# A two-layer hybrid decoder trunk in float32: split weight pairs kept in HBM, token shift on ScalarE, a quarter rope table, and a planner with other durations

## The chip, the cores and the metric

One core of a Trainium2 chip runs the whole program in one launch. The metric is the device time of one execution in microseconds (us). TensorE is called PE here, VectorE DVE, ScalarE ACT, GpSimd POOL; SP is the sync engine, which issues every DMA of this kernel, in one queue and in order.

## The reference

The input is x of 1024 tokens by 1024 features. Each of two layers does this:

```
h = rms_norm(x, g1)
pa, pb, pc = split(h @ w_in)          # 1024 -> 1056 + 768 + 448 columns
ya = rwkv7_mixer(pa)     # pa + (shift(pa) - pa) * mu, then a delta-rule recurrence over the tokens
yb = dilated_mixer(pb)   # rope on 16 of 64 features of q and k, three dilations, softmax
yc = mla_mixer(pc)       # low-rank q and kv, rope on 64 features, causal softmax
x = x + concat(ya, yb, yc) @ w_out
h = rms_norm(x, g2)
x = x + (silu(h @ w_gate) * (h @ w_up)) @ w_down
```

`shift` moves every feature one token later, with zero ahead of the first token. The rope tables are the cosine and the sine of position times a frequency: 8 frequencies for mixer B, 32 for mixer C, and the 8 of B are every fourth one of the 32 of C. A last norm follows the second layer.

## The kernel before, in words

Activations lie with features on the 128 partitions and half of the tokens (`HALF` = 512) along a row, so that a tile ("page", from a pool of 79) is 128 x 512 float32. A float32 product is made of three passes in the PE's faster float32r form (`mm3`): each operand is split into a high part (`wh`, by an ACT copy that rounds) and a low part (`wl` = value minus high part, by POOL or DVE), and high x high, high x low and low x high are summed in PSUM.

**Weights.** A weight matrix is read in units of 128 x 512 (256 KB), each worth 4 x 3 matmuls of 512 columns. `loader` has two strands: `fetch` reads raw units ahead (at most 3, `NRAW`), and the main loop splits them by `split(wr, wh, wl, "pool")` into a ring of 6 pairs (`NW`); `drop` gives a pair back when its last matmul has been emitted. The input projection (18 column blocks of two units, `in_items`) and the output projection (8 blocks of two units, `out_items`) are run for each half of the tokens, `hf` 0 and 1, and for each half every unit is read and split anew: 36 and 16 units per half and layer.

**The mixers.** `in_proj` runs the blocks of hf 0, then those of hf 1, and hands each block's PSUM bank on: `shifted` (blocks 0 to 8) does the token shift, `evac_to` the rest. In `shifted` ACT copies the bank to `raw` (in layer 0, hf 0 DVE does it with the norm's factor), then DVE makes `last - raw` for one column, `raw` shifted minus `raw` for 511 columns, and a scalar_tensor_tensor with `mu`. `recurrence(hf)` is a long serial chain over 8 chunks of 64 tokens that goes back and forth between PE, DVE and ACT: first an elimination of 31 steps (`Wp`, `tmp`, two small DVE operations each) between 32 x 1024 transposes on DVE (`vtrans`), which PE's `mg` matmuls wait for; then, chunk by chunk, `X` (PE), `Xs` (DVE), `U` (PE), `UV` (ACT), `Hp` (PE). The attention of B and C runs beside it and after it. Then come the output projection (`wo`) and the feed-forward part (`gu`, `dn`), which are long runs of 512-column matmuls.

**Rope.** `rope_tables(kind, hf)` makes cosine and sine on 128 x 512 for one kind of rope and one half; `all_rope` runs it four times, in layer 0, from the end of hf 0 on, and stores the four pairs in `rope_dram`. `load_rope` reads a pair back by two DMAs.

**Order.** All of this is written as Python generators ("strands"). A planner (`Flow`) picks the next instruction to emit by simulated clocks: `F.op(engine, cost)` advances an engine's clock by the planner's price of an operation, and `LATENCY` (150 ns after DVE, ACT or POOL, 230 ns after PE, 130 ns more where PE is the one that waits) is added from an operation to the next of its strand. Engines run their instructions in the order of emission, so a price that is off puts an instruction too early or too late in its engine's queue; SP's DMAs come in that order too. Prices before: a DVE operation of n columns costs 1.04 n + 65 ns, a DVE transpose 1.1 n + 65, an ACT copy 0.833 n + 80, POOL 2.2 n + 65, a float32r matmul max(n, 2m) x 0.4167 + 3, a float32 one 4 max(n, m) x 0.4167 + 6.

Of the kernel before, what the change touches and what calls it, by code (L numbers as in the profile page):

```python
# [18 lines left out]
L = 2  # L19
T = 1024  # L20
# [61 lines left out]
class Strand:  # L82
# [148 lines left out]
def trunk(ctx: ExitStack, tc: tile.TileContext, xT, pos, vec, con, first, w_in, small, uq, uqr, ukv,  # L231
# [45 lines left out]
    def activation(out, in_, func, bias=None, scale=None, accum_out=None):  # L277
        cost = cols(in_) * 0.833 + 80
        kw = {}
        for k, v in (("bias", bias), ("scale", scale), ("accum_out", accum_out)):  # L280
            if v is not None:
                kw[k] = v
                if not isinstance(v, float):
                    cost += 93
# [7 lines left out]
    def acopy(out, in_):  # L292
        F.op("act", cols(in_) * 0.833 + 80)
# [4 lines left out]
    def tt(eng, out, a, b, op):  # L298
        F.op(eng, cols(out) * (1.04 if eng == "dve" else 2.2) + 65)
        ENG[eng].tensor_tensor(out=out, in0=a, in1=b, op=op)  # L300

    def ts(out, in_, s1, s2, op0, op1=None, rate=0.55):
        F.op("dve", cols(out) * rate + 65)
# [3 lines left out]
    def stt(out, a, s, b, op0, op1):  # L307
        F.op("dve", cols(out) * 1.04 + 65)
        nc.vector.scalar_tensor_tensor(out=out, in0=a, scalar=s, in1=b, op0=op0, op1=op1)  # L309

    def vcopy(out, in_, rate=1.04):
        F.op("dve", cols(out) * rate + 65)
        nc.vector.tensor_copy(out=out, in_=in_)

    def recip(out, in_):
        F.op("dve", cols(out) * 8.33 + 65)
# [129 lines left out]
    afix = {"last": fix.tile([128, 9], F32, name="last")}  # L446
# [5 lines left out]
    rope_dram = drp.tile([2, 2, 2, 128, HALF], F32, name="rope_dram")  # L452
# [3 lines left out]
    rope_done = [[Event(), Event()] for _ in range(2)]  # L456
# [15 lines left out]
    raws, ring = Slots(NRAW), Slots(NW)  # L472
    at_layer = [0]

    def loader(items):

# [18 lines left out]
        queue = [(k, parts(k, srcs), own(k)) for k, srcs in items]  # L495
# [19 lines left out]
        for k, todo, keep in queue:  # L515
            if k[0] == "S":
# [13 lines left out]
            F.set(W[k], (wh, wl))  # L530
# [190 lines left out]
    def rope_tables(kind, hf):  # L721

        col = CON["rope"] + 3 * kind
        s = P["gp"]
# [4 lines left out]
        F.cur.last, F.cur.t = None, dma(q, pos[0:1, hf * HALF:(hf + 1) * HALF].partition_broadcast(128), 262144)  # L729
        yield "dve"  # L730
        vcopy(ang, q)
        free(q)
        yield "dve"
        ts(ang, ang, cons[:, col:col + 1], None, ALU.mult)
        yield "dve"
        ts(k, ang, 0.15915494309189535, 12582912.0, ALU.mult, ALU.add)
        yield "dve"
        ts(k, k, -12582912.0, None, ALU.add)
        for c in (-6.28125, -1.93500518798828125e-3, -3.0199157663e-7):
            yield "dve"  # L740
            stt(ang, k, c, ang, ALU.mult, ALU.add)
        yield "dve"
        ts(ang, ang, 3.1415925, -3.1415925, ALU.min, ALU.max)
        yield "act"
        activation(k, ang, ACTF.Sin)
        yield "dve"
        ts(k, k, cons[:, col + 1:col + 2], None, ALU.mult)
        yield "dma"
        t = dma(rope_dram[kind, hf, 1], k, 262144)
        free(k)  # L750
        yield "dve"
        stt(ang, ang, -1.0, ang, ALU.mult, ALU.max)
        yield "dve"
        ts(ang, ang, -1.0, 1.5707963267948966, ALU.mult, ALU.add)
        yield "act"
        activation(ang, ang, ACTF.Sin)
        yield "dma"
        t = dma(rope_dram[kind, hf, 0], ang, 262144)
        free(ang)
        F.set(rope_done[kind][hf], None, t)  # L760

    def all_rope():
        for kind in range(2):
            for hf in range(2):
                yield from rope_tables(kind, hf)

    def load_rope(kind, hf, where, ev, keep=0):
        yield rope_done[kind][hf]
        C, S = yield from pages(where, ["ropeC", "ropeS"], keep=keep)
        yield "dma"  # L770
        dma(C, rope_dram[kind, hf, 0], 262144)
        F.set(ev, (C, S), dma(S, rope_dram[kind, hf, 1], 262144))
# [25 lines left out]
    def group(g, where, scale, mask, score, vpass, emit_out, whole, later, end):  # L798
# [5 lines left out]
        def qtile(i4):  # L804
# [9 lines left out]
            for cc in range(nch):  # L814
                n = ns[cc]
                yield "dve"
                F.op("dve", n * 1.04 + 65)
# [149 lines left out]
    def layer(l):  # L967
# [67 lines left out]
        def shifted(hf, idx, p, r0=0, r1=128):  # L1035
            yield Need([rawa])
            raw = yield from page(["gp"], "raw", keep=room(1) if hf else 0)
            yield from evac(raw[r0:r1], p[r0:r1], hf, slice(r0, r1))
            if idx != 8:
                free(p)  # L1040
            if hf == 1:
                yield A[0][idx]
            last = afix["last"][r0:r1, idx:idx + 1]
            m = yield from page(["gp"], "pa", keep=room(1) if hf else 0)
# [5 lines left out]
            yield "dve"  # L1050
            stt(m[r0:r1], m[r0:r1], vcol(l, "mu", idx)[r0:r1], raw[r0:r1], ALU.mult, ALU.add)
            free(raw)
# [41 lines left out]
        def in_proj():  # L1094
            for hf in range(2):
                order = IN_ORDER[hf]
                for n_, idx in enumerate(order):
                    if hf == 0 and n_ == 4:
                        F.spawn(norm1(1), 4)
                    if l == 0 and (hf, n_) == ROPE_START:  # L1100
                        F.spawn(all_rope(), 7)
# [74 lines left out]

        def start_a():
            nc.vector.memset(afix["last"], 0.0)
# [32 lines left out]
        def recurrence(hf):  # L1211
# [88 lines left out]
            for j in range(2):  # L1300
# [13 lines left out]
                F.op("dve", 1130)  # L1314
# [1325 lines left out]
```

## Time and profile before

| | us |
|---|---|
| runs | 2668.68, 2671.2, 3381.49 |
| median | 2671.2 |
| the profiled execution's own time | 2675.43 |
| its span, first to last instruction | 2673.5 |
| PE busy in it | 2564.4 (96%) |
| DVE, POOL, ACT busy | 1822.3, 1269.6, 1154.0 |
| mean granted PE clock | 0.97 |
| moved by DMA | 365.09 MB, 137 GB/s |

The busy time of PE counts modelled ends of pipelined matmuls, so a stretch can be 100% busy without running at full pace; PEld is the time in which weights are loaded into PE's array, one load to a matmul. The granted clock has two levels here, 1.0 (2.4 GHz) and 0.5 (1.2 GHz); a row gives its mean over a stretch.

### The profile page before, as it was taken

The numbers are of one execution on the slowest core, as the hardware profiler recorded it, in microseconds if no ns is written. First come the engines' busy times: TensorE is split into PE (matmuls) and PEld (weight loads), VectorE is DVE, ScalarE is ACT, GpSimd is POOL, SyncE is SP. The second block draws the span as 40 slices with busy tenths as digits, with TensorE's granted clock in tenths as the row PEclk, the third lists the DMA queues.
The fourth block names the chain that finished last, engine by engine and source line by source line (L and its number), as shares of the span: only waits on it lengthen the run. The fifth ranks groups of instructions, "written<-read, shape, count | busy, mean of one in ns | idle before, by whom it ended". The sixth has DMA issues, their size and how long they took to land. (4 is left out here: it accounts for less than half of the span.)

```text
span 2673.5 us, 38613 instructions
## 1 busy us (share of the span) xinstructions
PE 2564.4 (96%) x13112; PEld 2053.2 (77%) x13112; DVE 1822.3 (68%) x3535; ACT 1154.0 (43%) x2319; POOL 1269.6 (47%) x978
## 2 busy tenths in 40 slices
PE   7999898999999999999999999999998999999998
PEld 5777765688777888888877778658887888888887
DVE  7978648674778666655578377677548876665556
ACT  5354346564433433332354434756634333333221
POOL 4635433146664444356564255213656444454660
PEclk9889888999999999999999998999999999999999
DMA  5231202015435443698342221111352554349851
GB/s 185 81 115 60 79 20 70 18 60 193 155 115 204 168 141 131 242 347 286 123 143 81 72 74 50 46 35 59 114 200 95 190 173 165 124 149 348 285 205 63
DMA packets 204773, 365.09 MB, mean 137 GB/s; under 512 B 23712, under 2 KB 38304, under 8 KB 204448
## 3 DMA queue, kind: packets, MB, share of 16 engines
q1 hardware_dynamic: 204576, 362.63, 39.8%
q8 instruction: 103, 1.69, 0.3%
q14 instruction: 94, 0.77, 0.1%
HBM read 253.22 MB, written 105.64 MB: 134 GB/s over the span
## 5 line engine op out<-in xcount | busy, mean ns | idle before, releaser
L300 POOL TENSOR_TENSOR wl<-wr,wh 128x512 fp32r<-128x512 f32 (+1 forms) x376 | 550.6, 1476 | 459.8 <-ACT wh L294 410.2
L265 PE MATMUL gu<-hhi,wh 128*128 128x512 f32 x1232 | 483.3, 393 | 18.6 <-ACT u L294 12.6
L265 PE MATMUL gu<-hhi,wl 128*128 128x512 f32 x1232 | 480.7, 391 | 1.2 <-POOL wl L300 1.0
L265 PE MATMUL gu<-hlo,wh 128*128 128x512 f32 x1232 | 481.2, 391 | 0.0
L294 ACT CAST wh<-wr 128x512 fp32r<-128x512 f32 (+1 forms) x496 | 287.2, 597 | 104.8 <-POOL wl L300 35.3
L265 PEld LDWEIGHTS gu<-hhi,wh 128*128 128x128 f32 x1232 | 232.3, 189 | 76.5 <-ACT u L294 15.1
L265 PEld LDWEIGHTS gu<-hhi,wl 128*128 128x128 f32 x1232 | 232.4, 189 | 51.1 <-POOL wl L300 2.5
L300 POOL TENSOR_TENSOR wl<-s,wh 128x512 fp32r<-128x512 f32 (+1 forms) x136 | 180.1, 1333 | 187.6 <-ACT wh L294 84.1
L265 PEld LDWEIGHTS gu<-hlo,wh 128*128 128x128 f32 x1232 | 232.4, 189 | 47.3
L265 PE MATMUL dn<-bhi,wh 128*128 128x512 f32 (+1 forms) x664 | 251.7, 380 | 0.7 <-issue 0.7
L265 PE MATMUL dn<-blo,wh 128*128 128x512 f32 (+1 forms) x664 | 251.5, 379 | 0.0
L265 PE MATMUL dn<-bhi,wl 128*128 128x512 f32 (+1 forms) x664 | 251.5, 379 | 0.0
L265 PE MATMUL inp<-hhi,wh 128*128 128x512 f32 x512 | 219.2, 428 | 9.3 <-ACT wh L294 9.3
L294 ACT CAST wh<-s 128x512 fp32r<-128x512 f32 (+1 forms) x204 | 116.7, 581 | 229.8 <-DVE s L300 199.7
L265 PE MATMUL inp<-hhi,wl 128*128 128x512 f32 x512 | 209.1, 408 | 0.3 <-POOL wl L300 0.3
L265 PE MATMUL inp<-hlo,wh 128*128 128x512 f32 x512 | 209.0, 408 | 0.0
L300 DVE TENSOR_TENSOR x<-x,dn 128x512 f32<-128x512 f32 (+1 forms) x160 | 104.4, 657 | 110.6 <-PE dn L265 82.1
L300 DVE TENSOR_TENSOR v<-u,gu 128x512 f32<-128x512 f32 x132 | 89.9, 682 | 127.8 <-PE gu L265 125.4
L300 POOL TENSOR_TENSOR v<-v 128x512 f32<-128x512 f32 x66 | 97.1, 1474 | 136.7 <-DVE v L300 126.4
L265 PEld LDWEIGHTS dn<-bhi,wh 128*128 128x128 f32 x664 | 124.9, 188 | 25.2 <-issue 1.5
L265 PEld LDWEIGHTS dn<-bhi,wl 128*128 128x128 f32 x664 | 124.9, 188 | 23.6
L265 PEld LDWEIGHTS dn<-blo,wh 128*128 128x128 f32 x664 | 124.9, 188 | 23.1
(316 smaller groups left out, 5500.8 us busy)
## 6 DMA issues: line engine op xcount, KB each, us to landing
wr<-in_w_in_dram SPq DMA_DIRECT2D x144, 256.0 KB
act_dram<-ahi SPq DMA_DIRECT2D x142, 256.0 KB
act_dram<-alo SPq DMA_DIRECT2D x142, 256.0 KB
bhi<-act_dram SPq DMA_DIRECT2D x142, 256.0 KB
blo<-act_dram SPq DMA_DIRECT2D x142, 256.0 KB
wr<-in_w_gate_dram SPq DMA_DIRECT2D x104, 256.0 KB
wr<-in_w_up_dram SPq DMA_DIRECT2D x104, 256.0 KB
wr<-in_w_down_dram SPq DMA_DIRECT2D x96, 192.0 KB
```

The source lines that it names most:

```text
L265: nc.tensor.matmul(out=out, lhsT=lhsT, rhs=rhs, start=start, stop=stop, **kw)
L294: nc.scalar.copy(out=out, in_=in_)
L300: ENG[eng].tensor_tensor(out=out, in0=a, in1=b, op=op)
```

## The change

Four things are done together.

1. **Weight pairs.** When a unit of `w_in` or `w_out` has been split for hf 0, both parts are also written to HBM (`pairs_dram`); for hf 1 they are read from there, straight into the ring, with no raw tile and no split.
2. **Token shift.** ACT reads the PSUM bank twice, times (1 - mu) and times mu (in hf 1 already moved by one column), and DVE adds the two. `last` holds mu times the last column. The vector `less` = 1 - mu is made once per layer in place of a memset.
3. **Rope table.** One table for 32 frequencies x 4 blocks of 256 tokens on 128 partitions: cosine, sine and minus sine. `load_rope` gathers both kinds from it, by 8 DMAs in place of 2; for B, POOL first fills the pages with 1 and 0.
4. **Planner prices.** New durations for every operation, and 35 ns in place of 150 from an operation to the next of its strand on the same engine.

```diff
         if self.last is None or (self.last == "pe" and self.want == "pe"):
             return self.t
+        if self.last == self.want:
+            return self.t + 35.0
         return self.t + LATENCY[self.last] + (EXTRA if self.want == "pe" else 0.0)
...
         if lhsT.dtype == F32R:
-            F.op("pe", max(n, 2 * m) * 0.4167 + 3)
+            F.op("pe", max(n + 32, 262) * 0.4167)
         else:
-            F.op("pe", 4 * max(n, m) * 0.4167 + 6)
+            F.op("pe", 2 * max(n + 20, m) * 0.4167 + 4)
...
     def acopy(out, in_):
-        F.op("act", cols(in_) * 0.833 + 80)
+        F.op("act", cols(in_) * 0.833 + 175)
...
     def tt(eng, out, a, b, op):
-        F.op(eng, cols(out) * (1.04 if eng == "dve" else 2.2) + 65)
+        F.op(eng, cols(out) * 1.2 + 150 if eng == "dve" else cols(out) * 2.5 + 120)
...
     def vtrans(out, in_):
-        F.op("dve", cols(in_) * 1.1 + 65)
+        F.op("dve", cols(in_) * 1.9 + 150)
...
+    def again(k):
+        return k[0] in ("in", "wo") and k[2] == 1
...
-        queue = [(k, parts(k, srcs), own(k)) for k, srcs in items]
+        queue = [(k, [] if again(k) else parts(k, srcs), own(k)) for k, srcs in items]
...
         for k, todo, keep in queue:
+            if again(k):
+                yield there[(*k[:2], 0, *k[3:])]
+                yield Need([ring])
+                w = yield from pages(["gp"], ["wh", "wl"], F32R, keep, 3.2)
+                at = pair(k)
+                yield "dma"
+                for i in range(2):
+                    t = dma(f32(w[i]), at[i], 262144)
+                F.set(W[k], w, t)
+                continue
...
             yield from split(wr, wh, wl, "pool")
             raw_free(wr)
-            F.set(W[k], (wh, wl))
+            now = F.cur.at()
+            if k[0] in pairs_dram:
+                yield "dma"
+                for i, w in enumerate((wh, wl)):
+                    t = dma(pair(k)[i], f32(w), 262144)
+                F.set(there[k], None, t)
+            F.set(W[k], (wh, wl), now)
...
-    def rope_tables(kind, hf):
+    def rope_tables():
...
+        col, n = CON["rope"] + 3, T // 4
...
+        C, S, N, q_ = ang[:, 0:n], k[:, 0:n], k[:, n:2 * n], q[:, 0:n]
         yield "dma"
+        for b in range(4):
+            t = dma(q_[32 * b:32 * b + 32], pos[0:1, b * n:(b + 1) * n].partition_broadcast(32), 32768)
...
+        for i, a in enumerate((C, S, N)):
+            t = dma(rope_dram[i], a, 131072)
...
+        if kind == 0:
+            for t, v in ((C, 1.0), (S, 0.0)):
+                yield "pool"
+                F.op("pool", 550)
+                nc.gpsimd.memset(t, v)
...
+        for i, a in enumerate(starts):
+            for t, v in ((C, src[0]), (S, src[1 if i % 2 else 2])):
+                done = dma(t[a:a + n].rearrange("p (q t) -> p q t", q=2), v, 2048 * n)
...
         def shifted(hf, idx, p, r0=0, r1=128):
...
+            d, m = yield from pages(["gp"], ["raw", "pa"], keep=room(1) if hf else 0)
+            src = p
+            if not (hf or l):
+                yield from evac(d[r], p[r], hf, r)
...
+            yield "act"
+            activation(m[r], src[r], ACTF.Copy, scale=rest)
...
+            yield "act"
+            if hf:
+                activation(d[r, 1:], src[r, 0:HALF - 1], ACTF.Copy, scale=mu)
+                acopy(d[r, 0:1], last)
+            else:
+                activation(d[r], src[r], ACTF.Copy, scale=mu)
+                acopy(last, d[r, HALF - 1:])
...
             yield "dve"
-            tt("dve", m[r0:r1, 0:1], last, raw[r0:r1, 0:1], ALU.subtract)
-            tt("dve", m[r0:r1, 1:], raw[r0:r1, 0:HALF - 1], raw[r0:r1, 1:], ALU.subtract)
-            if hf == 0:
-                vcopy(last, raw[r0:r1, HALF - 1:])
-            yield "dve"
-            stt(m[r0:r1], m[r0:r1], vcol(l, "mu", idx)[r0:r1], raw[r0:r1], ALU.mult, ALU.add)
-            free(raw)
+            if hf:
+                tt("dve", m[r], m[r], d[r], ALU.add)
+            else:
+                tt("dve", m[r, 1:], m[r, 1:], d[r, 0:HALF - 1], ALU.add)
+            free(d)
```

## Rows read from the trace of the kernel before

**Rows 1.** The page, engines' busy time (share of the span) and instructions:

```profile
PE 2564.4 (96%) x13112; PEld 2053.2 (77%) x13112; DVE 1822.3 (68%) x3535; ACT 1154.0 (43%) x2319; POOL 1269.6 (47%) x978
```

**Rows 2.** Busy time by stretch; last columns: granted clock, DMA share, GB/s:

```profile
core 0: us, PE busy (x) PEld busy (x) DVE busy (x) ACT busy (x) POOL busy (x), PEclk, DMA share, GB/s
14.00:160.00 146.00, 135.37 (x659) 110.32 (x658) 134.34 (x261) 64.45 (x107) 81.82 (x61) 0.95 0.36 123
160.00:400.00 240.00, 221.45 (x1608) 170.73 (x1607) 157.43 (x377) 108.44 (x211) 96.09 (x80) 0.88 0.18 59
400.00:620.00 220.00, 204.81 (x1046) 151.22 (x1045) 156.85 (x457) 139.06 (x344) 76.82 (x77) 0.95 0.17 54
620.00:700.00 80.00, 80.00 (x360) 66.37 (x359) 40.30 (x57) 34.55 (x61) 49.72 (x37) 1.00 0.63 211
1330.00:1900.00 570.00, 548.67 (x3312) 423.14 (x3311) 402.13 (x1018) 293.73 (x638) 242.59 (x210) 0.96 0.22 69
```

**Rows 3.** Waits of PE: who waited for whom, total us, times, longest:

```profile
PE mg L265 <- DVE T1Y L321: 9.3, 2, 8.2
...
PE hsum L275 <- DVE sq L313: 8.5, 7, 3.5
PE U L265 <- DVE Xs L313: 6.1, 5, 2.6
...
PE gu L265 <- POOL wl L300: 1.0, 1, 1.0
```

**Rows 4.** The same stretches view, 20 us around the longest of these waits:

```profile
290.00:300.00 10.00, 4.87 (x33) 4.33 (x31) 8.06 (x23) 2.12 (x4) 2.85 (x3) 0.85 0.79 265
300.00:310.00 10.00, 6.96 (x118) 6.56 (x119) 5.52 (x7) 2.11 (x4) 1.78 (x1) 0.50 0.08 16
```

**Rows 5.** DVE groups of the rope tables, costliest and cheapest of 8, 44 instructions:

```profile
L309 DVE SCALAR_TENSOR_TENSOR ang<-kr,ang 128x512 f32<-128x512 f32 x12 | 9.1, 762 | 0.0
...
L313 DVE CAST ang<-posi 128x512 f32<-128x512 int32 x4 | 1.7, 415 | 0.0
```

**Rows 6.** Groups of the token shift (busy us, mean ns | idle before):

```profile
L309 DVE SCALAR_TENSOR_TENSOR pa<-pa,vecs,raw 128x512 f32<-128x512 f32 (+1 forms) x36 | 35.4, 986 | 0.3
L300 DVE TENSOR_TENSOR pa<-raw 128x511 f32<-128x511 f32 (+1 forms) x36 | 25.6, 710 | 0.0
L300 DVE TENSOR_TENSOR pa<-last,raw 128x1 f32<-128x1 f32 (+1 forms) x36 | 15.1, 419 | 13.3 <-ACT raw L294 13.1
L294 ACT COPY raw<-inp 128x512 f32<-128x512 f32 (+1 forms) x27 | 15.8, 584 | 31.6 <-PE inp L265 31.5
```

**Rows 7.** Groups of the weight split on POOL and ACT, and a DVE transpose:

```profile
L300 POOL TENSOR_TENSOR wl<-wr,wh 128x512 fp32r<-128x512 f32 (+1 forms) x376 | 550.6, 1476 | 459.8 <-ACT wh L294 410.2 <-DVE x L300 17.4 <-issue 10.8
L294 ACT CAST wh<-wr 128x512 fp32r<-128x512 f32 (+1 forms) x496 | 287.2, 597 | 104.8 <-POOL wl L300 35.3 <-PE dn L265 18.5 <-POOL x L300 18.1
L321 DVE STREAM_TRANSPOSE TT<-W 32x1024 f32<-32x1024 f32 x8 | 18.3, 2287 | 2.5 <-ACT W L294 2.5
```

**Rows 8.** Timeline of SP, one DMA issue: start us, us:

```profile
24.09 0.40 SPq L328 DMA_DIRECT2D swt<-in_small_dram  x1
```

**Rows 9.** DMA issues of the input projection's weights, count and size:

```profile
wr<-in_w_in_dram SPq DMA_DIRECT2D x144, 256.0 KB
```

**Rows 10.** The stretches view again, where DMA is busiest in the projections:

```profile
20.00:30.00 10.00, 7.17 (x37) 5.84 (x38) 7.14 (x19) 3.75 (x9) 3.66 (x3) 1.00 0.76 269
30.00:40.00 10.00, 9.91 (x48) 8.00 (x46) 9.89 (x15) 6.68 (x12) 7.78 (x6) 1.00 1.05 384
620.00:640.00 20.00, 20.00 (x90) 16.57 (x89) 10.27 (x11) 10.88 (x20) 14.08 (x10) 1.00 0.78 275
```

**Rows 11.** Waits of SP's queue, 160 to 300 us, then 1450 to 1700 us:

```profile
SPq L328 <- DVE kr L305: 59.6, 3, 22.6
SPq L328 <- DVE yA L300: 18.9, 1, 18.9
...
SPq L328 <- PE Yp L265: 25.9, 1, 25.9
SPq L328 <- DVE yA L300: 25.3, 2, 22.8
```

More of the change, by code (lines that the diff above doesn't have):

```diff
@@ L298, in tt @@
     def tt(eng, out, a, b, op):
-        F.op(eng, cols(out) * (1.04 if eng == "dve" else 2.2) + 65)
+        F.op(eng, cols(out) * 1.2 + 150 if eng == "dve" else cols(out) * 2.5 + 120)
         ENG[eng].tensor_tensor(out=out, in0=a, in1=b, op=op)
     def ts(out, in_, s1, s2, op0, op1=None, rate=0.55):
-        F.op("dve", cols(out) * rate + 65)
+        F.op("dve", cols(out) * rate + 180)
         kw = {} if op1 is None else {"op1": op1}
@@ L445, in trunk @@
     pj_dram = drp.tile([10, 128, HALF], F32, name="pj_dram")
-    afix = {"last": fix.tile([128, 9], F32, name="last")}
+    afix = {"last": fix.tile([128, 9], F32, name="last"), "less": fix.tile([128, 9], F32, name="less")}
     for i in range(2):
@@ L455, in trunk @@
     xs_done = [[Event(), Event()] for _ in range(KD)]
-    rope_done = [[Event(), Event()] for _ in range(2)]
+    rope_done = Event()
     flip = [0]
@@ L472, in trunk @@
     raws, ring = Slots(NRAW), Slots(NW)
+    pairs_dram = {"in": drp.tile([L, 18, 2, 2, 128, HALF], F32, name="pairs_in"),
+                  "wo": drp.tile([L, KD, 2, 2, 128, HALF], F32, name="pairs_wo")}
     at_layer = [0]
+    def again(k):
+        return k[0] in ("in", "wo") and k[2] == 1
+    there = {}
     def loader(items):
+        there.update({k: Event() for k, _ in items if k[0] in pairs_dram})
         def keep(k):
@@ L493, in parts, with pair @@
             return [(Event(), srcs[g][b], g, b) for g, b in at]
[L495 removed]
+        def pair(k):
+            return pairs_dram[k[0]][k[1], k[3], k[4]]
+        queue = [(k, [] if again(k) else parts(k, srcs), own(k)) for k, srcs in items]
         def fetch():
@@ L750, in rope_tables @@
-        free(k)
-        yield "dve"
[L752 to L756, printed above, removed]
-        yield "dma"
[L758 to L772, printed above, removed]
+        stt(C, C, -1.0, C, ALU.mult, ALU.max)
+        yield "dve"
+        ts(C, C, -1.0, 1.5707963267948966, ALU.mult, ALU.add)
+        yield "act"
+        activation(C, C, ACTF.Sin)
+        yield "dve"
@@ new lines, in rope_tables, with load_rope @@
+        ts(N, S, -1.0, None, ALU.mult)
+        yield "dma"
+        for i, a in enumerate((C, S, N)):
+            t = dma(rope_dram[i], a, 131072)
+        free(ang, k)
+        F.set(rope_done, None, t)
+    def load_rope(kind, hf, where, ev, keep=0):
+        yield rope_done
+        C, S = yield from pages(where, ["ropeC", "ropeS"], keep=keep)
+        rows = slice(64 * hf, 64 * hf + 64)
+        if kind == 0:
[3 more added lines that the diff above has]
+                nc.gpsimd.memset(t, v)
+            src = [rope_dram[i, rows].rearrange("(q g r) t -> r g q t", q=2, r=4)[0] for i in range(3)]
+            n, starts = 8, (0, 8, 64, 72)
+        else:
+            src = [rope_dram[i, rows].rearrange("(q f) t -> f q t", q=2) for i in range(3)]
+            n, starts = 32, (0, 32, 64, 96)
+        yield "dma"
+        for i, a in enumerate(starts):
+            for t, v in ((C, src[0]), (S, src[1 if i % 2 else 2])):
+                done = dma(t[a:a + n].rearrange("p (q t) -> p q t", q=2), v, 2048 * n)
+        F.set(ev, (C, S), done)
@@ L1175, in open_a @@
             F.set(a_open)
+        less = afix["less"]
         def start_a():
-            nc.vector.memset(afix["last"], 0.0)
+            o = l * NVEC + VEC["mu"]
+            ts(less, vecs[:, o:o + 9], -1.0, 1.0, ALU.mult, ALU.add)
         def load_swt():
```

57 lines of the change are left out of this document (28 added, 29 removed).

## The prediction

> **What bounds the kernel now.** I read the page's busy times first, then the stretches, then who makes PE wait, and last the groups that the change touches. The page shows PE busy in 2564.4 of 2673.5 us [rows 1]: at most 109.1 us are plain idle, and no other engine is near full. The stretches tell where. In 620 to 700 us (the output projection) PE has no idle time, runs at clock 1.00 and does 360 matmuls in 80 us, 222 ns each [rows 2]; that is its pace when it is fed. The two mixer stages are different. In layer 0 (14 to 620 us) PE idles 606 - 561.6 = 44.4 us, and the clock of 0.95, 0.88 and 0.95 takes another 146 x 0.05 + 240 x 0.12 + 220 x 0.05 = 47.1 us of full pace; in layer 1 (1330 to 1900 us) it is 21.3 us idle and 570 x 0.04 = 22.8 us by the clock [rows 2]. Together the mixers lose 65.7 + 69.9 = 135.6 us. The other 43.4 us of idle time lie at the start, at the two entries of the feed-forward part and in the last norm, which the change hardly touches. So what can be won is a part of 135.6 us, or 5%, and nothing that only lightens POOL or ACT wins by itself.
>
> The Trainium skill, "Perfetto Trace Analysis", section "Identifying the Most-Contended Engine", says that matmul busy time is a poor measure of the room left and that the share of weight loading is a better one. Here that share is 66.37 / 80 = 0.83 where PE is fed; at this share the loads of the two mixer stages would fill 521 of 606 and 510 of 570 us, a room of 145 us against 65.7 by the idle time [rows 2]. By it a third of the room is 48 us, by the idle time alone 22.
>
> The waits show what the loss is made of. PE's `mg` waits 9.3 us for the elimination's last DVE transpose, `hsum` 8.5 us for a DVE copy, `U` 6.1 us for `Xs` on DVE; a split `wl` on POOL makes `gu` wait 1.0 us [rows 3]. Around the longest wait PE is busy in only 4.87 of 10 us, and the next 10 us run at 0.50 [rows 4]: one wait of 8.2 us is paid again at half clock. PE's loss in the mixers is mostly lateness of DVE's links in the recurrence, met by matmuls that stand too early in PE's queue.
>
> **The change, part by part.** The sum is made against the profiled execution, 2675.4 us, which is 4.2 us above the median of the runs (2671.2).
>
> *Rope table.* Out go 44 DVE instructions in eight groups, of which the first and the last are shown; the eight sum to 30.1 us [rows 5]. In come 11 on 256 columns; each is priced at the cheapest row's 415 ns at most, so 4.6 us. DVE gains 25.5 us, nearly all in 160 to 400 us. PE loses (18.6 + 28.8) / 240 = 20% of that stretch [rows 2]; taking DVE's time to be on the path in that share gives 5 us. Ends: 0 (the strand has the lowest priority and fills gaps) and 25.5. DMAs: 4 position loads, 8 stores and 16 loads become 4, 3 and 64, 43 more issues of 0.40 us [rows 8], 17 us of SP's time spread over two layers; SP is not on the path and the weights' lead hides them, so I take 0, with 17 as the end if the lead is gone. Eight fills on POOL, even at the 1476 ns of a split, make 12 us [rows 7] on an engine that is busy 40% of that stretch: 0.
>
> *Token shift.* A shift takes 0.986 + 0.710 + 0.419 us of DVE now [rows 6]; one sum like the 0.710 stays, so 1.4 us go, 36 times: 50.6 us, half in each layer. By PE's lost share (91.5 / 606 = 15% in layer 0, 44.1 / 570 = 8% in layer 1) that is 3.8 + 2.0, say 6 us; ends 0 and 50.6. ACT gains 27 x 1 + 9 x 2 = 45 passes of 584 ns [rows 6], 26 us, and 36 copies of one column, between 0 and another 21 us; it loses 104 splits of 597 ns, 62 us [rows 7]. So ACT is lighter in the end and delays nobody; a PSUM bank is kept one pass longer, which four spare banks cover.
>
> *Weight pairs.* Of the 144 raw units of the input projection [rows 9] half are not split again, and 16 of the output projection in each layer: 104 in all, 153 us of POOL and 62 us of ACT [rows 7]. PE waits for these splits so little [rows 3] that this is worth 1 us. The price is in DMA: 208 stores and 208 loads of 256 KB for 104 loads, 82 MB on top of 365, and 312 issues. A unit feeds 12 matmuls, 2.67 us, so hf 0 writes 0.524 MB per 2.67 us = 196 GB/s. At the start some 10 units are used by 40 us and 6 stand in the ring: 8.4 MB, 22 us at the highest rate seen, 384 GB/s, with room for 3 us of it at 20 to 30 us [rows 10]. So weights could come up to 19 us late there. Filled, the lead is 8 units (3 raw, 5 split), 21 us, which would hide all of it; at the start it is only being built. I take 8 of 0 to 19. At the output projection 275 + 196 = 471 GB/s would be asked for, 87 above 384, over 16 units or 43 us: 9.7 us late per layer, inside the lead, so 0, with 19 as the end for two layers.
>
> The Trainium skill, "DMA: Bandwidth & Descriptors", section "Specifications", puts a core's limit at HBM at about 358 GB/s, which speaks against this part. The 384 GB/s of the row is above it [rows 10], so the measurement decides; by 358 the lateness at the output projection would be an estimated 13.6 us per layer, still inside the lead.
>
> For hf 1 the lead shrinks: no raw tiles, 5 pairs behind the one in use, 13.3 us. Behind a store that waits, SP issues no weights. It stood 22.6 us at a rope store and 18.9, 25.9 and 22.8 us at others [rows 11]. The rope stores' 59.6 us go; the other three exceed the new lead by 5.6 + 12.6 + 9.5 = 27.7 us. In these stretches PE interleaves the recurrence with the projection, which stretches the lead, so I take 0, with 27.7 as the end.
>
> *Planner prices.* Before, a 32 x 1024 transpose was planned at 1191 ns and took 2287, a split's POOL half at 1191 and took 1476, ACT's half at 506 and took 597, a DVE sum at 597 and took 710 [rows 6, 7]; a 512-column matmul at 216 and took 222 [rows 2]. So the plan had DVE's links ready too soon, and PE's dependent matmuls stand too early. The new prices (2096, 1400, 601, 764, 227) are near the rows. The three waits of the kind that a later place in the queue fills with projection matmuls make 23.9 of 65.7 us, 36% [rows 3]; with the clock that follows them [rows 4] I take a third of what is left after the terms above, (135.6 - 12) / 3 = 41 us. Ends: the 23.9 us once more as a loss, since all queues are dealt anew, and two thirds, 82, as a gain. The long runs of matmuls outside the mixers have no idle time to win and their queue has one natural order: 0.
>
> Sum: -5 - 6 - 1 + 8 - 41 = -45 us: 2630 us profiled, 2626 us as a median.
>
> **The rivals.**
>
> *The order gives two thirds.* If nearly every wait in the mixers is a misplaced matmul, PE stays fed and the clock stays up: -90 + 8 = -82, 2589 us. For it: after the longest wait half clock doubles the loss [rows 4]. Against: `Xs`, `UV` and `Hp` are links of one serial chain, and late in each mixer no projection is left to fill its gaps.
>
> *The relief is off the path.* POOL and ACT were not waited for, DVE's waits are latency and not load, and a dealt-anew queue meets as many late links as the old one: 2671.2 - 12 + 8 = 2667 us. For it: DVE was busy 92% only in 14 to 160 us, 66% in 160 to 400 [rows 2].
>
> *SP's queue starves hf 1.* The place is the second half of the input projection; the mechanism is a store of something late ahead of pair loads that have only the ring as lead; it decides from the point where SP stands longer than 13.3 us. Price: 27.7 there, 19 at the start and 19 at the output projections, 66 us, against 12 us of relief and no gain by order: 2725 us. Against it: hf 1 uses units more slowly than one per 2.67 us.
>
> **How the numbers follow.** The forecast (2605 to 2650 us) has 0.41, the larger gain 0.28, the relief off the path 0.22, starving 0.09. A difference under about 2% (53 us) counts as no change here: the bounds are 2618 and 2725 us. Faster: 0.28 and the lower part of the forecast, 0.11, so 0.39. Slower: half of the starving case, 0.05. Between: 0.56. The range 2572 to 2682 leaves out the far end of the large gain (0.05), the upper part of the relief case (0.04) and starving (0.09).
>
> **What would show it.** Right: the waits of `mg`, `hsum` and `U` sum to under 12 us; the clock of the stretch that answers to 160 to 400 us rises above 0.93; DVE's busy total falls by some 70 us and POOL's by some 150; SP no longer stands at `kr`. The DMA term is right if `inp` waits a few us for DMA or `wh` in the first 60 us and `wo` for nothing. Wrong: PE waiting for `wh` by DMA in hf 1, new waits of the same size in the recurrence, or a feed-forward part that changes its length.

## The result, and the profile after

The changed kernel takes 2686.8 us (median), 1.0057 times the kernel before (95% interval 1.0036 to 1.0077): 0.6% longer where I had forecast 1.7% shorter, and above the upper end of my range. The ratio is of fast runs, so the single 3381.49 us of the kernel before is not in it. The profiled execution of the changed kernel took 2683.0 us with a span of 2681.2 us, 7.7 us more than before's 2673.5. The medians differ by about 15 us, so what is read from these two executions, the balance by stage above all, holds about half of the loss.

The page of the changed kernel: the engines' busy time, and what DMA moved.

```profile
PE 2561.3 (96%) x13112; PEld 2053.6 (77%) x13112; DVE 1759.7 (66%) x3414; ACT 1122.1 (42%) x2281; POOL 1086.6 (41%) x882
...
DMA packets 249624, 442.73 MB, mean 165 GB/s; under 512 B 29136, under 2 KB 46800, under 8 KB 249296
```

Against [rows 1] DVE has 62.6 us less work, POOL 183.0, ACT 31.9. PE is busy 3.1 us less in a span 7.7 us longer, so its idle time rose from 109.1 to 119.9 us. Three engines were relieved, and the one that bounds the kernel, PE, idles more.

The changed kernel's stretches (columns as in rows 2); the first four answer to [rows 2], 290 to 300 to [rows 4].

```profile
14.00:160.00 146.00, 128.91 (x623) 102.98 (x622) 118.59 (x222) 70.07 (x122) 66.74 (x53) 0.94 0.72 251
160.00:400.00 240.00, 233.02 (x1727) 179.19 (x1725) 136.28 (x380) 104.11 (x221) 63.48 (x63) 0.95 0.31 99
400.00:620.00 220.00, 207.60 (x1050) 156.91 (x1051) 144.17 (x424) 134.47 (x330) 79.21 (x79) 0.95 0.25 86
1330.00:1900.00 570.00, 547.01 (x3327) 423.17 (x3326) 376.89 (x982) 291.29 (x644) 198.07 (x182) 0.97 0.35 116
...
290.00:300.00 10.00, 10.00 (x119) 9.23 (x118) 3.82 (x3) 1.32 (x3) 0.00 (x0) 1.00 0.68 240
...
50.00:60.00 10.00, 4.70 (x17) 3.05 (x16) 5.02 (x11) 9.46 (x12) 2.88 (x4) 0.94 0.08 31
...
620.00:640.00 20.00, 17.77 (x79) 14.39 (x77) 6.38 (x9) 4.92 (x9) 4.33 (x4) 1.00 1.01 358
640.00:660.00 20.00, 17.39 (x71) 14.00 (x72) 15.53 (x30) 7.00 (x12) 7.20 (x6) 0.83 0.77 278
```

In layer 0 the change did win, in 160 to 400 us: PE's busy time went from 221.45 to 233.02 and the granted clock from 0.88 to 0.95, 11.6 + 240 x 0.07 = 28 us of full pace. The hole at 290 us is gone: PE is busy there for 10.00 of 10 us at clock 1.00. In 14 to 160 us it lost 6.5 us of busy time, and in layer 1 the stretch as a whole is what it was.

The waits of PE over the whole run of the changed kernel (us in total, times, longest), answering to [rows 3]:

```profile
PE gu L267 <- ACT u L296: 19.9, 6, 6.0
PE inp L267 <- ACT wh L296: 18.4, 3, 8.8
PE ssum L267 <- DVE sq L302: 14.4, 7, 4.1
PE ssum L277 <- DVE ry L311: 13.0, 8, 3.8
PE tp L277 <- ACT P L292: 6.9, 8, 2.1
PE gu L267 <- ACT ahi L296: 5.6, 2, 2.8
PE Hp L267 <- ACT UV L292: 3.7, 7, 0.8
...
PE U L267 <- DVE Xs L315: 1.6, 3, 1.0
PE hsum L277 <- DVE sq L315: 1.4, 2, 0.7
```

The waits that I had made the sign of success, `mg`, `hsum` and `U`, fell from 23.9 to 3.0 us (`mg` has no row left). Their place was taken: `gu` for ACT's `u` went from 12.6 to 19.9, `inp` for ACT's `wh` from 9.3 to 18.4, `ry` from 9.2 to 13.0, `tp` for `P` from 1.2 to 6.9, `Hp` for `UV` from 0.8 to 3.7. The named waits gave up 20.9 us, and these five, for which my sign of success had no place, took 28.8.

The balance by stage makes it plain. The stages are timed from the first matmul of one to the first of the next, in the profiled executions; us:

| stage | before | after | difference |
|---|---|---|---|
| mixers, layer 0 | 602.9 | 580.0 | -22.9 |
| output projection, layer 0 | 90.5 | 101.5 | +11.0 |
| gate and up products, layer 0 | 436.9 | 443.5 | +6.6 |
| mixers, layer 1 | 562.8 | 561.7 | -1.1 |
| output projection, layer 1 | 94.1 | 103.3 | +9.2 |
| gate and up products, layer 1 | 438.0 | 442.1 | +4.1 |

With +0.8 in the rest the sum is +7.7 us. Two questions follow. Why did the stages outside the mixers, which I had put at nothing, lose 31 us? And was the mixers' gain the work of the prices, which my sum made its largest term?

### The profile page after: what moved, and what is told of

Same layout as the page of the kernel before. It is cut to its first block, busy times and chain, and to the rows that moved or that the text cites. A ratio compares the mean times of both kernels' runs of the same rounds, so it can differ in the third digit from the quotient of the medians.

```text
span 2681.2 us, 38950 instructions
## 1 busy us (share of the span) xinstructions
PE 2561.3 (96%) x13112; PEld 2053.6 (77%) x13112; DVE 1759.7 (66%) x3414; ACT 1122.1 (42%) x2281; POOL 1086.6 (41%) x882
## 4 chain that ended last, share of the span: by engine, by line
PE 73%; DVE 10%; issue 9%; POOL 4%; ACT 2%; DMA 1%; SPq 0%; POOLq 0%; DVEq 0%; ACTq 0%
PE gu L267 26%; PE dn L267 16%; PE inp L267 7%; PE wo L267 6%; PE o L267 4%; PE sc L267 4%; PE tp L277 2%; POOL wl L302 1%; PE Yp L267 1%; PE X L267 1%; DVE P L859 1%; DVE hx L302 1%; PE vB L267 1%; DVE hlo L302 1%; DVE rt L302 1%
## 5 line engine op out<-in xcount | busy, mean ns | idle before, releaser
L302 POOL TENSOR_TENSOR wl<-wr,wh 128x512 fp32r<-128x512 f32 (+1 forms) x272 | 370.3, 1372 | 383.9 <-ACT wh L296 336.3
L267 PE MATMUL gu<-hhi,wh 128*128 128x512 f32 x1232 | 485.8, 395 | 26.0 <-ACT u L296 19.9
L296 ACT CAST wh<-wr 128x512 fp32r<-128x512 f32 (+1 forms) x392 | 225.8, 591 | 90.4 <-POOL wl L302 35.2
L267 PE MATMUL inp<-hhi,wh 128*128 128x512 f32 x512 | 216.0, 422 | 18.4 <-ACT wh L296 18.4
```

The lines of the kernel that those rows point to most:

```text
L296: nc.scalar.copy(out=out, in_=in_)
```

## The experiments

Each run was timed beside the kernel before, whose median was 2669.6 to 2671.6 us there; a ratio is to that kernel. Old prices are those of the kernel before.

### Parts against prices

**The prices alone** (`prices_alone`), in the kernel before, all of them and the rule for a strand that stays on its engine:

```diff
+        if self.last == self.want:
+            return self.t + 35.0
...
-        F.op("dve", cols(in_) * 1.1 + 65)
+        F.op("dve", cols(in_) * 1.9 + 150)
...
```

> The kernel before with the new planner prices alone. Theory 1 (the prices lay the queues of the output projection, of the entry of the feed-forward part and of the attention worse, and lose what the other parts win): 2680 to 2700 us, and the output projection and the entry show PE waiting for DVE sq and ACT u as in the changed kernel. Theory 2 (the weight pairs fill the DMA queues at the output projection, about 10 us in each layer, and the prices win in the mixers): 2640 to 2655 us, the output projection 90 and 94 us long as before.

2708.8 us, 1.0135 (1.0113 to 1.0156), slower than either theory had it. The term that I had at -41 us is +37 by itself. Its longest wait of PE, and two stretches, the first around that wait:

```profile
PE mg L267 <- DVE T1Y L323: 19.6, 1, 19.6
```

```profile
318.00:340.00 22.00, 2.36 (x35) 1.92 (x34) 17.69 (x36) 10.07 (x17) 4.47 (x4) 0.63 0.16 60
340.00:380.00 40.00, 39.06 (x329) 31.20 (x327) 6.03 (x16) 11.64 (x27) 4.34 (x6) 0.50 0.01 1
```

The input projection of layer 0 ended at 318 us, against 400.9 before. The second half's elimination came after that, and no projection matmul was left for its gap: PE did 2.4 us of work in 22, then ran 40 us at clock 0.50 (1.2 GHz).

**The three parts at old prices** (`parts_old_prices`): weight pairs, shift and rope table in, all price lines back to the old ones.

> The weight pairs, the token shift and the rope table with the old planner prices. Theory 1: 2640 to 2655 us, since the projections win some 20 us and nothing is laid worse. Theory 2: 2680 to 2695 us, since DMA at 350 GB/s or more delays both output projections by some 10 us each and nothing is won by order.

2665.4 us, 0.9974 (0.9959 to 0.9989), between the two theories. From here to the changed kernel the prices cost 21.3 us. The mixers of layer 0 take 571.2 us here and 580.0 in the changed kernel, 602.9 before: their gain is there without the prices, which answers the second question.

**Without the pairs** (`without_pairs`), the changed kernel with every unit split again:

```diff
     def again(k):
-        return k[0] in ("in", "wo") and k[2] == 1
+        return False
```

(The edit takes the pairs' buffers and stores out too.)

> The changed kernel without the weight pairs: every unit is read and split anew for the second half. Theory 1: 2675 to 2690 us, near the changed kernel, since the prices stay. Theory 2: 2655 to 2667 us; the output projections come back to 91 and 94 us and DMA falls from 350 to about 275 GB/s there.

2673.0 us, 1.0006 (0.9993 to 1.0019), again between the theories. All pairs together cost 13.8 us.

**Pairs for the input projection only** (`pairs_input_only`), the changed kernel with:

```diff
-        return k[0] in ("in", "wo") and k[2] == 1
+        return k[0] == "in" and k[2] == 1
```

> The changed kernel with weight pairs for the input projection alone, the output projection's units are read and split anew. Theory 1: within 5 us of the changed kernel (2687). Theory 2: 2665 to 2670 us, the output projections 91 and 94 us long, and the waits of ssum for DVE sq at their middle (3.3 and 4.1 us) gone.

2667.7 us, 0.9985 (0.9969 to 1.0001): 19.1 us less than with both kinds. The second theory held: the output projections are back at 93.8 us each, `ssum` no longer waits in their middle, and so the pairs of the output projection are the loss there.

**The output projection's pairs alone** (`out_pairs_only`), in the kernel before, old prices; `again` returns `k[0] == "wo" and k[2] == 1`.

> The kernel before with pairs for the output projection alone, old prices. If the stores fill DMA there whatever the prices: 2680 to 2692 us, both output projections about 10 us longer (100 and 104 us), DMA near 350 GB/s in their first half. If the lead hides them, as the prediction had it: within 4 us of the kernel before.

2681.8 us, 1.0042 (1.0023 to 1.0061): 11 us longer, with the output projections at 96.5 and 103.4 us. The first theory had the time right. Its stretches there, then who makes DVE and PE wait (640 to 712 us, layer 1's 1940 to 2000 us, and PE's of 611 to 712 us):

```profile
611.00:631.00 20.00, 20.00 (x90) 16.55 (x89) 3.89 (x4) 6.40 (x12) 11.45 (x9) 1.00 0.99 336
631.00:651.00 20.00, 20.00 (x90) 16.57 (x89) 6.12 (x9) 5.22 (x9) 5.11 (x4) 1.00 1.00 348
651.00:671.00 20.00, 17.26 (x72) 12.84 (x70) 11.47 (x28) 8.47 (x15) 6.34 (x5) 0.91 1.06 400
...
1948.00:1968.00 20.00, 15.49 (x65) 12.22 (x64) 9.51 (x21) 3.75 (x6) 2.56 (x2) 0.84 1.03 384
```

```profile
DVE x L300 <- DMA x<-in_xT_dram: 13.1, 3, 4.8
...
DVE x L300 <- DMA x<-xs_dram: 7.2, 2, 4.7
...
PE ssum L265 <- DVE sq L300: 2.2, 1, 2.2
```

DMA is full for 60 us (share 0.99 to 1.06), where the kernel before asked for 275 GB/s [rows 10]. Some of the residual's tiles `x`, which stand in the same queue, come late, and DVE's adds wait for them. But that is not what stops PE. These are the last add of the first half and PE's `ssum` of the norm behind it, in `out_pairs_only` and then in the kernel before (start us, us):

```profile
656.54 0.69 DVE L300 TENSOR_TENSOR x<-x,wo 128x512 f32<-128x512 f32 x1 [2.87 <-PE wo L265]
658.73 1.05 PE L265 MATMUL ssum<-cons,sq 128*128 128x1 f32 x8 [2.23 <-DVE sq L300]
```

```profile
658.01 0.69 DVE L300 TENSOR_TENSOR x<-x,wo 128x512 f32<-128x512 f32 x1 [3.37 <-PE wo L265]
660.53 0.95 PE L265 MATMUL ssum<-cons,sq 128*128 128x1 f32 x8
```

In both kernels the last add waits for PE's own product and not for a load, and `ssum` comes 2.2 and 2.5 us after it. The difference is what PE has to do in that time. A half of the tokens has 8 x 2 x 12 = 192 `wo` matmuls. In the kernel before 204 of them stand ahead of `ssum`, so 12 of the second half fill the gap; here exactly 192 do, and PE stops. It is so in every trace here: in the four kernels that keep pairs of the output projection 192 stand ahead, in both layers, and `ssum` waits 2.2 to 4.4 us; in all others 204 or 207, with no wait. After the stop part of the stretch runs at 0.91 and 0.84, and the stage takes 96.3 to 104.0 us in these four against 90.0 to 94.1 in the others. In the rows of the kernel before, PE has no idle time from 620 to 700 us [rows 2].

The second half's weights are hardly what is late, at least in layer 0 of the changed kernel: their first pair was asked for at 626.67 and 627.14 us, ahead of `x` tiles asked for at 631.85 which DVE had added by 638.5, while `ssum` waited until 641.06. DVE had stood idle for 7.5 us before the first of these two adds, so its `x` probably was late, and the wait is 3.3 us in place of 2.2. What has changed in all four kernels is PE's order: a pair can be read back only after it has been stored, and the plan set the second half's products behind the norm. That the planner's own account of the full DMA queue made it do so is argued, not shown.

**The best of these** (`best_guess`): shift, rope table and input pairs, old prices, no output pairs.

> Old prices, token shift, rope table and pairs for the input projection alone. If the prices' loss (21 us between the two kernels with all three parts) and the loss of the output projection's pairs (19 us under the new prices) are two things that add, this one is 2645 to 2655 us, faster than both kernels. If the output projection's pairs cost only under the new prices, it is near the three parts with the old prices, 2660 to 2668 us.

2649.7 us, 0.9919 (0.9899 to 0.9938), as the first reading had it: the two losses add. The medians now make a chain: 2671.5 before; -21.9 for these three parts; +18.0 for the prices (2667.7); +19.1 for the output pairs (2686.8).

### Which prices

**Only the two matmul prices** (`pe_prices_only`), on `best_guess`:

```diff
-            F.op("pe", max(n, 2 * m) * 0.4167 + 3)
+            F.op("pe", max(n + 32, 262) * 0.4167)
...
-            F.op("pe", 4 * max(n, m) * 0.4167 + 6)
+            F.op("pe", 2 * max(n + 20, m) * 0.4167 + 4)
```

> As the kernel with old prices and pairs for the input projection alone, with the new prices of the two kinds of matmul and all others old. Theory A (the lower price of the float32 matmuls makes the plan see PE free during the chains, so the projection's matmuls are used up early and none are left for the second recurrence): 2665 to 2680 us, the input projection of layer 0 ends before 325 us, and the granted clock after it falls to 0.90 or less. Theory B (the prices of DVE, ACT and POOL do it): within 6 us of the kernel with old prices.

**All the others** (`other_prices_only`), on `best_guess`: every new price and the 35-ns rule, but the two lines above left old.

> The same with all new prices except those of the matmuls. Theory A: within 6 us of the kernel with old prices. Theory B (longer links of DVE, ACT and POOL in the plan make it put more of the projection's matmuls into each gap): 2665 to 2680 us with the input projection of layer 0 ended before 325 us.

2685.2 us (1.0047) and 2670.0 us (0.9995): +35.6 and +20.4 on 2649.7, while both together are +18.0. The two halves do not add, and neither of my two theories held: the first named its projection to end before 325 us and it ended at 361.9, with a time above the range it gave; the second hit the time, but the projection ended at 337.6. With the matmul prices alone the gate and up products took 446.0 and 446.1 us instead of 436.9. PE's waits there, 686 to 1133 us:

```profile
PE gu L265 <- DVE v L300: 8.4, 6, 1.4
PE gu L265 <- ACT wh L294: 7.6, 2, 4.4
```

In the kernel before these two are 1.0 and 0.2 us. So "the long runs outside the mixers: 0" was false: their links to ACT and DVE are dealt anew like all others. The changed kernel shows it too, and not by chance of one deal. With all new prices `gu` waits 19.8 to 19.9 us for ACT's `u` in each of four kernels (`after`, `pairs_input_only`, `without_pairs`, `prices_alone`), and in the first three the gate and up products take 442.1 to 443.5 us per layer; the same parts at old prices (`parts_old_prices`, `best_guess`, `shift_and_rope`) have 10.2 to 13.2 us of that wait and 436.9 to 438.4. That is 9 to 12 us of the 18 to 21 that the prices cost there.

**The 35-ns rule alone** (`same_engine_35`), in the kernel before: the two lines that are first in this section's first diff, and nothing else.

> The kernel before with the planner's rule of 35 ns in place of 150 between two operations of a strand on one engine, no other price changed. If this rule carries the prices' loss (a chain on DVE then looks shorter than it is, since the old operation prices left out some 100 ns each): 2690 to 2710 us. If it doesn't: within 10 us of the kernel before.

2737.0 us, 1.0241 (1.0216 to 1.0266), the slowest of all. **The changed kernel without that rule** (`after_without_35`):

> The changed kernel without the rule of 35 ns between two operations of a strand on one engine (150 again), all else as changed. Margin theory: 2660 to 2678 us, below the changed kernel (2687), the larger margin on top of the new prices. If the rule only corrects what the new operation prices contain: 2685 us or more, since chains then look longer than they are.

2691.8 us, 1.0087 (1.0071 to 1.0104). Alone the rule costs 65 us, above the range that I gave it; in the changed kernel it saves some 5. Without it the gate and up products come back to 438.2 and 436.5 us, and the mixers take 27 us more. Nothing that it does can be priced apart from the other prices.

### The small terms, one at a time at old prices

> The kernel before with the one rope table alone, old prices. The prediction's terms: 5 us less, 2665. Theory R (the gain of some 28 us in the mixers of layer 0, which layer 1 does not show, is the rope table's, since layer 1 makes no table): 2640 to 2655 us, all of it between the start and the output projection of layer 0.

> The kernel before with the token shift on ACT alone, old prices. The prediction's terms: 6 us less, 2665, 4 in layer 0 and 2 in layer 1. Theory R: within 5 us of before, since layer 1 has shifts too and won nothing.

> The kernel before with pairs for the input projection alone, old prices. The prediction's terms: 1 us less and up to 8 more at the start, 2671 to 2678. Theory R: within 5 us of before; the other two kernels with and without these pairs differed by 5 us.

> The token shift and the rope table at old prices, no weight pairs. If their gains add (21 and 12 us alone): 2636 to 2642 us, the fastest so far. If a part of each is a lucky deal: 2645 to 2660 us.

| kernel | us | ratio (95%) |
|---|---|---|
| `rope_alone` | 2659.7 | 0.9955 (0.9937 to 0.9973) |
| `shift_alone` | 2650.4 | 0.9911 (0.9893 to 0.9930) |
| `in_pairs_alone` | 2666.0 | 0.9973 (0.9961 to 0.9984) |
| `shift_and_rope` | 2654.3 | 0.9931 (0.9910 to 0.9951) |

Each is faster alone, by 12, 21 and 5 us, and the sum would be 38; the three together gave 21.9, and shift with rope table 17, less than the shift alone. That rope was the bearer of the gain fell, and none of the three times is the one that the prediction's terms gave (2665, 2665, 2671 to 2678). A part of each number is probably not the saved work: in the profiled executions `rope_alone` has 558.6 us of mixers in layer 1 against 562.8, though the tables are made in layer 0.

### How much is the deal

These change no instruction of the kernel, only numbers that the planner puts the queues in order by:

```diff
-BIAS = 30.0
+BIAS = 45.0
```

```diff
-LATENCY = {"pe": 230.0, "dve": 150.0, "act": 150.0, "pool": 150.0}
+LATENCY = {"pe": 230.0, "dve": 200.0, "act": 200.0, "pool": 200.0}
```

The first is `bias_45`; the second, in the kernel before, is `latency_200`, and on `best_guess` it is `best_with_200`; `latency_160` has 160.0 in the three places.

> The kernel before with one number of the planner changed that no operation's price depends on: the bias against strands of lower priority is 45 ns in place of 30. The instructions are the same, only their order moves. Theory D (any new deal of the queues moves the time by 10 us or more): outside 2665 to 2678 us. Theory E (the time hangs on the prices in a systematic way): within 6 us of the kernel before.

> The kernel before with the planner's latency after DVE, ACT and POOL at 160 ns in place of 150, nothing else. Theory D: 10 us or more away from 2671, to either side. Theory E: within 6 us.

> The kernel before with the planner's latency after DVE, ACT and POOL at 200 ns in place of 150, nothing else. Margin theory: 2640 to 2662 us, at or below the kernel with 160 (2662), with the waits of mg, U and hsum in sum below the 23.9 us of before. Draws: anywhere within 20 us of 2671, above 2671 as likely as below.

> Old operation prices, token shift, rope table, pairs for the input projection alone, and the latency at 200 ns. Margin theory: 2630 to 2645 us, below the 2650 of the same kernel with 150. Draws: 2650 with 15 us to either side.

| kernel | us | ratio (95%) |
|---|---|---|
| `bias_45` | 2673.5 | 1.0013 (0.9998 to 1.0029) |
| `latency_160` | 2661.9 | 0.9955 (0.9937 to 0.9973) |
| `latency_200` | 2634.3 | 0.9868 (0.9853 to 0.9883) |
| `best_with_200` | 2686.7 | 1.0058 (1.0038 to 1.0078) |

A longer assumed latency makes the kernel before 35 us faster and `best_guess` 37 us slower. So the idea behind the later two runs, that a margin on every link is what helps, fell with the second of them. The ranges for a mere draw, 20 us and 15 us to either side, were too narrow as well. `bias_45` stayed within the 6 us of Theory E, and `latency_160`, 10 us away, fell between its two theories. `latency_200`, the kernel before with three numbers changed, is the fastest version here, ahead of both kernels.

The difference lies in the mixers. In layer 0 they take 602.9 us before and 565.6 in `latency_200`, in layer 1 562.8 and 556.3; in `best_guess` 574.6 and 567.0, in `best_with_200` 598.4 and 584.5. The kernels before, `latency_200`, `best_guess` and `best_with_200`, 330 to 460 us, with the input projection ended at 400.9, 355.6, 342.7 and 347.4 us, so that only the last two hold about the same work:

```profile
330.00:460.00 130.00, 116.14 (x636) 79.52 (x636) 82.93 (x249) 72.87 (x163) 43.66 (x34) 0.86 0.14 43
330.00:460.00 130.00, 128.25 (x763) 81.88 (x764) 91.88 (x313) 85.12 (x206) 34.33 (x30) 0.97 0.14 42
330.00:460.00 130.00, 120.75 (x673) 80.62 (x672) 92.91 (x310) 86.34 (x205) 39.96 (x31) 0.87 0.14 41
330.00:460.00 130.00, 116.39 (x636) 77.37 (x634) 84.13 (x240) 72.14 (x166) 40.71 (x34) 0.79 0.14 39
```

`latency_200` keeps PE busy for 128.25 of 130 us at clock 0.97. `best_with_200` idles 13.6 us there, 4.4 more than `best_guess`, and runs at 0.79 in place of 0.87, which costs another 130 x 0.08 = 10.4 us of full pace. What is added in idle time is paid again by the clock, here more than twice over.

## Why the prediction was wrong, point by point

**What bounds the kernel: right for the mixers, and too narrow.** PE's idle time and half clock in the mixers were a loss that could be won back, and 277 us less work on three other engines did not shorten the span, with the prices changed as well: it ended 7.7 us later. But what the mixers won, 24 us, the stages outside them, set at nothing, lost again and 7 us more.

**The planner's prices (-41): the step that failed.** The step read the new prices as truer, concluded that PE's dependent matmuls would stand later, and took a third of the mixers' loss as won. Measured, the prices cost 37 us alone, 18.7 on shift and rope table (`without_pairs` against `shift_and_rope`), 18.0 on shift, rope table and input pairs, and 21.3 on all parts: the same sign four times. My end for a loss, 23.9 us, holds three of the four; the forecast had its sign the other way. Three things were wrong in it.

First, I took shown durations for the time that an engine is taken. Back-to-back instructions in the timeline of the kernel before (start us, shown us), two on DVE and two on ACT:

```profile
302.93 0.64 DVE L300 TENSOR_TENSOR pj<-pj,sw 128x512 f32<-128x512 f32 x1
303.50 0.67 DVE L300 TENSOR_TENSOR pj<-pj,ropeC 128x512 f32<-128x512 f32 x1
...
427.63 0.58 ACT L294 COPY ph<-tp 128x512 f32<-128x512 f32 x1
428.11 0.62 ACT L294 CAST hhi<-hx 128x512 fp32r<-128x512 f32 x1
```

DVE's second starts 0.57 us after the first, though 0.64 is shown; ACT's 0.48 after, though 0.58 is shown. Over the whole trace such DVE sums start 603 ns apart (median of 533 pairs, 683 shown), ACT's casts 521 ns apart (619 shown), POOL's halves of the split 1256 (1296 shown). The old prices were 597, 506 and 1191; the new ones are 764, 601 and 1400. For these the old prices were nearer, and I had called the new ones "near the rows"; only the DVE transpose, 1191 planned and 2287 shown, was far off. The Trainium skill, "Perfetto Trace Analysis", section "Optimizing Scalar/DVE Operations", notes of an instruction's access overhead that the profiled latency holds about twice the busy part, because the half for the write acknowledgement overlaps with the next instruction. This trace agrees, by 80 ns on DVE and 98 on ACT. That this tail makes the new prices cost time is argued, not shown, and it can't be all of it. The matmul prices did come nearer: 227 ns for 512 columns in place of 216, where starts stand 227 ns apart when PE is fed, and 111 in place of 219 for a matmul of `ssum`, where they stand 112 ns apart. These two alone (`pe_prices_only`) cost 35.6 us. So the premise that truer prices give a better order did not hold here.

Second, I counted only the waits that a later place would fill, and not what fills them. In `prices_alone` the projection's matmuls were used up 83 us earlier, and the gap of `mg`, 9.3 us in all before, became 19.6 with 40 us of half clock behind it. An early end of the projection is not the loss by itself: in the changed kernel it comes 68 and 21 us earlier than before, in `best_guess`, which is the faster, 58 and 34.

Third, I held one deal of the queues to be better than another by its reasons, and the stages outside the mixers to have only one. The rival "a dealt-anew queue meets as many late links as the old one" had this right in kind; it is what the trace after shows. But it had the loss at nothing, and its 2667 us were 20 too few.

**The output projection's pairs (0 of 0..19): the second step that failed.** I worked out the excess demand, 471 GB/s against 384, and then hid it in the weights' lead. No row shows a `wo` matmul waiting for a load, as I had it, and the stage was longer all the same. I had asked when the weights arrive and not what stands in PE's queue: the pairs took the second half's 12 matmuls away from ahead of the norm's `ssum`, and PE stopped there. The price was 11 us alone, 15.8 on `best_guess` at old prices, 19.1 at new ones: the upper end of my own bounds, reached by another way.

**Start of the input projection (+8): right in place and size, regained later.** PE's busy time in 14 to 160 us fell from 135.37 to 128.91 us, and the pairs are the cause: it is 136.06 in `without_pairs`, which has shift, rope table and prices, and 126.42 in `in_pairs_alone`, which has none of them. (The shift alone, at old prices, has less too, 131.18.) The way was not only the one that I gave. In 40 to 50 us DMA is full (share 1.00), but the longest wait of PE from 14 us on comes after it, in 50 to 60 us, where PE did 4.70 us of work, DMA was busy for a share of 0.08 and ACT for 9.46 us. The changed kernel's waits of 50 to 100 us, and ACT's two largest groups from 49 to 59 us:

```profile
PE inp L267 <- ACT wh L296: 9.6, 2, 5.3
ACT pa L292 <- DVE raw L302: 8.0, 2, 4.8
```

```profile
L292 ACT ACT_TABLE_LOAD x4 | 5.1, 1283 | 0.5 <-DVE cs L1373 0.5
L292 ACT ACTIVATE sg<-lo,vecs 128x512 f32<-128x512 f32 x4 | 2.7, 686 | 0.0
```

In that first wait, 5.3 us, the split's ACT half stood behind the sigmoids and exponentials of the recurrence and the table loads between them, of 1.28 us each; in the second, 4.3 us, behind the shift's new pass on ACT, which waited for `raw` on DVE. I had written that ACT "delays nobody", counting its load and not its order. By the end the loss is made up: the input pairs by themselves gained 5 us, where I had a loss of 7 with them.

**SP's lead in hf 1 (0 of 0..27.7): held.** No row shows PE waiting there for `wh` by DMA, and from 160 to 400 us PE is busy 97% of the time. The long stand behind `yA` is still there, 22.6 us, and reaches 30.0 us in layer 1, beyond the 13.3 us that I had as the lead, without a wait of PE for it. `kr` on DVE is gone from SP's waits; 5.9 us for `kr` on ACT are left. From 160 to 300 us:

```profile
SPq L330 <- DVE yA L302: 22.6, 1, 22.6
```

**Rope table (-5) and token shift (-6): right in sign, small in size.** Alone they measured -12 and -21 us, inside my ends of 25.5 and 50.6, but with the doubt below. DVE's work fell by 62.6 us, where 76 were counted; the sums that stay take 801 ns and not 710, which is 3.3 us of it. One of the two groups that the shift leaves on DVE, and the split on POOL, in the changed kernel (busy us, mean ns, idle before):

```profile
L302 DVE TENSOR_TENSOR pa<-pa,raw 128x511 f32<-128x511 f32 (+3 forms) x36 | 28.7, 801 | 23.7 <-ACT raw L292 11.5 <-ACT raw L296 8.2 <-DMA wh<-pairs_in 3.6
...
L302 POOL TENSOR_TENSOR wl<-wr,wh 128x512 fp32r<-128x512 f32 (+1 forms) x272 | 370.3, 1372 | 383.9 <-ACT wh L296 336.3
```

The splits on POOL went from 376 to 272, the 104 that I had counted.

**The signs I named.** They came (`mg`, `hsum`, `U` under 12 us, the clock above 0.93, DVE 62.6 less for some 70, POOL 183.0 for some 150, no `kr` on DVE, `wo` waiting for nothing), and the kernel was slower. They tested whether the named waits go. They did not test whether PE's idle time goes, and that sum, 109.1 to 119.9 us, is the one that I should have named. The signs of being wrong came as well: new waits of the same size, and feed-forward parts of another length.

**What stays open.** Changes of a few planner numbers, with no instruction added or removed, moved these kernels by -35 (`latency_200`), -10 (`latency_160`), +37 (`latency_200`'s numbers on `best_guess`), +65 (`same_engine_35`) and +2 us (`bias_45`). Against that a single -12 or -21 us cannot be divided into saved work and luck of the order, nor can all of the +18 us of the prices be called a property of those prices, though their sign held in every pairing tried and 9 to 12 us of it, in the gate and up products, came in each of them but `prices_alone`, which had half of that. For the output pairs the stage that lengthened is the stage that was touched, and PE's order and wait go with the pairs in every trace; that one is shown.

## What to carry to other kernels

Where each engine runs a fixed queue that a planner has put in order, a changed price or a removed instruction deals all the queues anew; run a few re-deals that change nothing else before a small gain is put down to the part itself. The time that an operation takes from its engine is the distance between the starts of back-to-back instructions, not the shown duration; but a truer price is not by itself a better order, so try the order. Where operands are stored and read back, ask not only whether the bandwidth of the stage holds them, but which matmuls filled the gaps of that stage before, and whether they can still stand there.

## What the runs showed of the hardware

A single core moved 400 GB/s, reads and writes mixed, for 20 us (`out_pairs_only`, 651 to 671 us), with the busy share of its DMA engines at 1.06. The Trainium skill, "DMA: Bandwidth & Descriptors", section "Specifications", has about 358 GB/s as a core's limit at HBM; here one core ran alone, and the measurement decides.

One wait was followed by a long stretch at half clock: after 22 us with 2.36 us of matmuls, `prices_alone` ran 40 us at 0.50 with PE busy 39.06 of them. The clock did not come back within that stretch, though PE was hardly ever idle in it; most of its 329 matmuls are the small ones of the recurrence.
